# All output gates as seven-product pairs, a shorter queue of plain blocks beside the scan, and the scan's skip moved to a group's end

## The chip, the cores and the metric

The kernel runs on one core of a Trainium2 chip. The metric is the device time of one execution in microseconds, as the median of the runs; a profile of one execution comes with it. All times below are microseconds unless they are marked ns.

## The reference, cut to what matters

One layer of a hybrid decoder runs for a prompt of 1024 tokens and 8 sample tokens. The two are processed side by side as one matrix of 1032 columns (tokens), with the model dimension of 1024 on the partitions in 8 tiles of 128. Three mixers read the same normalised input through one projection `w_in`:

```python
sc_b, sc_c, sc_x, z, xbc, dt_raw, q, gates = jnp.split(xn @ w_in, splits, axis=-1)
y_a = (sc_b * conv_u) @ w_sc_out
y_ssd, ssm_new = ssd_fn(xs, dt, a, bm, cm, ssm_s0)
y_ssd = (y_ssd + ssm_d[:, None] * xs).reshape(bsz, seq, SSM_D_INNER) * jax.nn.silu(z)
y_b = group_rmsnorm(y_ssd, ssm_norm_w, SSM_GROUPS) @ w_ssm_out
y_c = jnp.einsum('bhlm,bmhd->blhd', probs, mem_v).reshape(bsz, seq, ATTN_DIM) @ w_attn_o
g_a, g_b, g_c = jnp.split(jax.nn.sigmoid(gates), N_BRANCHES, axis=-1)
merged = g_a * y_a + g_b * y_b + g_c * y_c
```

The term `ssm_d * xs` is the skip. The state-space scan (`ssd_fn`) has 4 groups of 8 heads and, for the prompt, 8 chunks of 128 tokens; the sample's tokens take a recurrent step of their own. A feed-forward part and norms follow.

## The kernel before, in words

All matrix products are of fp32 precision, made of three products of fp32r parts (`hi`, `lo`). A **block** is one tile of 128 output columns of a weight, for all 1032 tokens. It is computed in one of two forms. `gemm` (line 203 is its matmul) takes a **plain block**: 8 input tiles x 3 parts x 3 column slices of 344, 72 matmuls. `strassen` (line 248, through `st_prod`) takes a **pair** of blocks with seven half-sized products instead of eight: 168 matmuls of 258 columns. It reads sums of the input's tiles (the forms `T1`, `nT2`, `T4`, half of them in the pool `xfx`) and writes its outputs into tiles `u` of the pool `pxa`; both pools lie at the right end of the on-chip memory and are closed by `pa_stack.close()`.

Of the 24 gate blocks, `gate_pair` computes numbers 0 to 19 as ten pairs, the last of them `gate_pair(18, plain)`, which ends this part of the kernel. Each gate goes through a `Sigmoid` and is stored to `gt_d`. The sample's recurrent steps (`with_steps`) run beside the earlier pairs. Then come two queues of plain blocks, in this order:

- `fillers`: 8 blocks of the attention's query (`q_step`) and the 4 last gates (`gate_step`, 20 to 23), 12 in all;
- `outs`: 24 blocks of output projections in three rounds of 8, `wo0m` from the short convolution (`sc_d`), `wo1m` and `wo2m` from the two halves of the state-space output (`yb_d`). Eight blocks `wo3m` of the attention's output (their results are `po3m`) follow; they read `at_d`.

A queue `pend` holds small pieces of other work. `gemm` takes `pace[0]` of them per block, spread over its eight steps (one for each input tile). At the seam between two rounds, `out_ahead` loads the next round's eight input tiles and `split_act` splits them, during the last block of the round before.

**The scan** is the first such queue. For each group: load its tiles `x` and `bc`, then for each chunk three pieces (`first`, `third`/`decay`/`prep`, `second`), then `z_pieces`, `group_norm`, and the store to `yb_d`. In a chunk, `load` brings the rows `r` from `ac_d`; `prep` makes decay factors of them on ScalarE; `first` transposes (`bp`, `xp`) and multiplies `r` with `cbm`; `second` computes `po` (from the state `s`) and `py`, sums them into `yt`, and adds the skip to `x` in four small operations (line 950); `third` updates the state through `pss`. Four PSUM uses a chunk share two small buffers. `s_skip` adds the sample's skip. The tiles of the scan come from one pool `ssd`, opened at the right end after `pa_stack` is closed. The pace is `len(pend) / (len(fillers) + KD)`: the pieces are spread over 20 blocks.

**The attention** is the second queue: 69 pieces at `pace[0] = 5`, with the sample's attention, the convolution states, and last `s_back`, which writes the sample's attention result into `at_d` (its transposes are `psob`, line 1509). After it the rest of `outs` runs without pieces.

The framework orders each engine's instructions itself, by program order and by readiness in its own model; a tile whose buffer is taken waits for the last user. On an engine, and on the SP and ScalarE queues of transfers, instructions run in the order that results.

Of the kernel before, what the change touches and what calls it, by code (L numbers as in the profile page):

```python
# [9 lines left out]
F32 = mybir.dt.float32  # L10
F32R = mybir.dt.float32r
AF = mybir.ActivationFunctionType
ALU = mybir.AluOpType
# [4 lines left out]
P = 128  # L18
D = 1024
T = 1024  # L20
NS = 8
TT = T + NS
# [4 lines left out]
KD = D // P  # L27
EPS = 1e-6
LAG = 3
GROUPS = 4  # L30
HEADS = 32
HPG = 8
# [5 lines left out]
C_SCB, C_SCC, C_SCX, C_Z, C_XBC, C_DT, C_Q, C_G = 0, 1024, 2048, 3072, 5120, 8192, 8224, 9248  # L38
# [3 lines left out]
def tile_kernel(ctx: ExitStack, tc, a, o):  # L42
    nc = tc.nc
    V, S, G, PE, SY = nc.vector, nc.scalar, nc.gpsimd, nc.tensor, nc.sync
# [111 lines left out]
    def ev_tile(name, shape=(P, TT + 4), dt=F32):  # L156
        return ev.tile(list(shape), dt, tag="ev", name=name)
# [8 lines left out]
    pend = deque()  # L166
# [12 lines left out]
    pace = [3, 0.0]  # L179
# [29 lines left out]
    def wblock(w, col):  # L209
        return w[:, col : col + P].rearrange("(k p) c -> p k c", p=P)  # L210
# [174 lines left out]
    w_in = a["w_in"][0]  # L385
# [3 lines left out]

    ph1 = ExitStack()  # L390
    cn = ph1.enter_context(tc.tile_pool(name="cn", bufs=1))
    h_sc = cn.tile([P, 8, 16], F32, tag="h_sc", name="h_sc")
    h_xc = cn.tile([P, 24, 24], F32, tag="h_xc", name="h_xc")
    xn = [(act_tile("ah", f"xnh{k}"), act_tile("al", f"xnl{k}")) for k in range(KD)]
    xw = [act_tile(("ah", "al")[k % 2], f"xw{k}", F32) for k in range(KD)]
    ps_dt, ps_b0 = mm_ps("ps_dt"), mm_ps("ps_B0")
# [140 lines left out]
    dtT = cn.tile([P, 9, HEADS], F32, tag="dtT", name="dtT")  # L537
    decst = cn.tile([P, NCK, HEADS], F32, tag="decst", name="decst")
    cdec = cn.tile([P, NCK, HEADS], F32, tag="cdec", name="cdec")
    dts = cn.tile([P, 16, NS], F32, tag="dts", name="dts")  # L540
    es = cn.tile([P, 16, NS], F32, tag="es", name="es")
    dpar = cn.tile([P, 16], F32, tag="dpar", name="dpar")
    ys = cn.tile([P, 16, NS], F32, tag="ys", name="ys")
    bcs = cn.tile([P, GROUPS, NS, 2], F32, tag="bcs", name="bcs")

    dt_stack = ExitStack()
    pd_ = dt_stack.enter_context(tc.tile_pool(name="pdt", bufs=1))
# [96 lines left out]
    def proj(col, name):  # L644
        return gemm(weights(wblock(w_in, col), "w" + name), xn, "ps_" + name)
# [65 lines left out]

        return [Step(wblock(w_in, C_Q + i * P), f"wq{i}", s)]

    def gate_step(i):
        def s():
            ps = proj(C_G + i * P, f"g{i}")
            t = ev_tile(f"g{i}")
            S.activation(t3(t), flat(ps), AF.Sigmoid)
            S.dma_start(gt_d[i], t[:, :TT])

        return [Step(wblock(w_in, C_G + i * P), f"wg{i}", s)]

    def xbc_conv(ct, u, name):
        G.memset(u[:, 0:3], 0.0)
        G.tensor_copy(tail_xc[:, ct // 8, :, ct % 8], u[:, T : T + 11])
# [58 lines left out]
    def gate_pair(i, after_t3=None):  # L784
        plain_pair(C_G, gt_d, i, "G", AF.Sigmoid, None, after_t3)
# [5 lines left out]
    def b3(t, n):  # L791
        return t.rearrange("p (a b) -> p a b", a=n)

    def sp_tile(shape, tag, name, bufs=2):
        return pool["ssd"].tile(shape, F32, tag=tag, bufs=bufs, name=name)


    def bc_rows():
# [67 lines left out]
        pair()  # L866
        assert not pend

    def ssd_pieces(g, xg, bcg):
        hs = slice(g * HPG, (g + 1) * HPG)  # L870
        h0 = g * HPG
        state = {}
# [4 lines left out]

        def load(c):
            nm = f"{g}_{c}"
            r = sp_tile([P, HPG, P], "r", "r" + nm, 3)  # L880
            live[c] = r
            SY.dma_start(r, ac_d[g, c].unsqueeze(0).to_broadcast([P, HPG, P]))

# [7 lines left out]
        def load_ea(c):  # L891
            ea = None
            if c > 0:
                ea = sp_tile([P, 4, P], "ea", f"ea{g}_{c}")
                for k in range(2):
                    SY.dma_start(ea[k * 64 : (k + 1) * 64], ea_d[g, c, 4 * k : 4 * k + 4].unsqueeze(0).to_broadcast([64, 4, P]))
            return ea
# [27 lines left out]
        def second(c):  # L925
            nm = f"{g}_{c}"
            cs = slice(c * P, (c + 1) * P)
            r, ea, xdt, xdd, bT = live[c]
            yt = sp_tile([P, 4, P], "yt", "yt" + nm, 1)
            if c > 0:  # L930
                po = sm_ps("po" + nm)
                for t in range(4):
                    PE.matmul(  # L933
                        po[:, t * P : (t + 1) * P], state["s"][:, t * P : (t + 1) * P], bcg[1][:, cs],
                        start=True, stop=True,
                    )
# [12 lines left out]
            for t in range(4):  # L949
                V.scalar_tensor_tensor(  # L950
                    xg[t][:, cs], xg[t][:, cs], dpar[:, g * 4 + t : g * 4 + t + 1], yt[:, t, :],
                    op0=ALU.mult, op1=ALU.add,
                )

        def third(c):
            nm = f"{g}_{c}"
            r, ea, xdt, xdd, bT = live.pop(c)
            pss = sm_ps("pss" + nm)
            PE.matmul(pss, bT, xdd, start=True, stop=True)  # L959
            if c == 0:  # L960
                s_new = sp_tile([P, 512], "s", "s" + nm)
                ins = V.tensor_copy(s_new, pss)
            else:
                s_new = state["next"]
                ins = V.tensor_tensor(s_new, pss, s_new, op=ALU.add)  # L965
            state["s"] = s_new
            return ins.ins

        def decay(c):

            s_new = sp_tile([P, 512], "s", f"s{g}_{c}")
            G.tensor_tensor(  # L972
                b3(s_new, HPG), b3(state["s"], HPG), bc(cdec[:, c, hs].unsqueeze(2), [P, HPG, 64]),
                op=ALU.mult,
            )
            state["next"] = s_new

        def final():
            ps = sm_ps(f"psf{g}")
            for t in range(4):  # L980
                PE.transpose(ps[:, t * P : (t + 1) * P], state["s"][:, t * P : (t + 1) * P], ident)
            sf = sp_tile([P, 4, P], "yt", f"sf{g}", 1)
            S.copy(sf, b3(ps, 4))
            SY.dma_start(
                o["p_ssm"][0, 0, hs].rearrange("h p n -> (h p) n").rearrange("(t q) n -> q t n", q=P), sf
            )

        def s_skip():
            for t in range(4):
                V.scalar_tensor_tensor(  # L990
                    xg[t][:, T:TT], xg[t][:, T:TT], dpar[:, g * 4 + t : g * 4 + t + 1], ys[:, g * 4 + t, :],
                    op0=ALU.mult, op1=ALU.add,
                )

        def head():
            load(0)
# [39 lines left out]
    def z_pieces(g, xg, hold):  # L1036
        def piece(t):
            zs = hold.pop(t)
            V.tensor_mul(xg[t], xg[t], zs)
            if t == 0:  # L1040
                hold["q"] = ev_tile(f"sqa{g}")
            sqa = hold["q"]
            if t == 0:
                S.activation(sqa[:, :TT], xg[t], AF.Square)
            else:
                S.activation(zs, xg[t], AF.Square)
                V.tensor_add(sqa[:, :TT], sqa[:, :TT], zs)
# [208 lines left out]
    with_steps(3, lambda: z_pair(14))  # L1256
    with_steps(2, lambda: gate_pair(16))
    assert not steps
    rb = ev_tile("rb")
    SY.dma_start(rb[:, :TT], r_d.to_broadcast([P, TT]))  # L1260
    b12s = []
# [17 lines left out]
        for kt in range(4):  # L1279
            split_to(*xforms["T3"][kt], b12s[kt // 2][:, HS[kt % 2]])  # L1280

    gate_pair(18, plain)
    st_stack.close()
    pa_stack.close()
    pmm[0] = mm_stack.enter_context(tc.tile_pool(name="pmm1", bufs=2, space=PSUM))


    pool["ssd"] = ssd.enter_context(tc.tile_pool(name="ssd", bufs=2, side="right"))
    fillers = deque()
    for i in range(8):  # L1290
        fillers.extend(q_step(i))
    for i in range(20, 24):
        fillers.extend(gate_step(i))

    acts = []

# [65 lines left out]
        )  # L1362
    for g in range(GROUPS):
        xg, bcg, hold = groups[g]
        pieces = ssd_pieces(g, xg, bcg)
        if g > 0:
            pend.extend([lambda g=g: load_group(g), None])
        pend.extend(pieces[:-3])
        pend.append(lambda g=g, hold=hold: [z_load(g, t, hold) for t in range(2)])
        pend.extend(pieces[-3:])  # L1370
        pend.extend(z_pieces(g, xg, hold) + [None] + group_norm(g, xg, hold))
    pace[0] = len(pend) / (len(fillers) + KD)
    while fillers or pend:
        if len(fillers) == 1:
            out_ahead(sc_d)
# [25 lines left out]
    if True:  # L1401
# [194 lines left out]
        pend.extend(pieces)  # L1596
        pend.extend(states)
        pend.extend([None, s_back])
        pace[0] = 5
        while pend:  # L1600
            run_next(outs)
        pace[0] = 3
        att_stack.close()
        ph2 = ctx.enter_context(tc.tile_pool(name="ph2", bufs=1))
        assert not pend
# [339 lines left out]
```

## Time and profile before

| | |
|---|---|
| median of 3 runs | 2502.28 us (2502.19 to 2504.86) |
| the profiled execution's own time | 2503.04 us |
| its span in the profile | 2501.3 us |
| busy, share of the span | TensorE 98%, weight loads 96%, VectorE 61%, ScalarE 42%, GpSimd 5% |
| transfers | 392.08 MB, mean 157 GB/s |
| pairs before the scan; scan; attention; merge and feed-forward | to 966; 966 to 1357; 1357 to 1567; from 1567 us |

The span is what lies between the first and the last instruction of the profile; the execution's own time is 1.7 us longer. A share of busy time is a mean over stages. The rows further down are copied from the page and from answers of the trace.

### The profile page before, as it was taken

How to read it: one execution, taken by the hardware profiler on the slowest of the kernel's cores; microseconds unless marked ns; L12 is line 12 of the kernel's file. 1: busy time of each engine (PE TensorE's matmuls, PEld its weight loads, DVE VectorE, ACT ScalarE, POOL GpSimd, SP SyncE). 2: the span in 40 equal slices, each digit the busy share in tenths (PEclk: the TensorE clock that was granted, in tenths of full speed). 3: DMA queues.
4: the chain of work that ended last, by engine and by line, in shares of the span. 5: the costliest groups of instructions: out<-in, count | busy, mean ns of one | idle time of the engine just before them, and what ended most of it. 6: DMA issues, size and time to landing. Idle time of an engine off the chain costs nothing.

```text
span 2501.3 us, 44971 instructions
## 1 busy us (share of the span) xinstructions
PE 2461.6 (98%) x18714; PEld 2399.9 (96%) x18714; DVE 1519.3 (61%) x2590; ACT 1047.0 (42%) x1688; POOL 135.3 (5%) x163
## 2 busy tenths in 40 slices
PE   7999999999999999999999999999999999999998
PEld 6999999999999998999989998999999999999998
DVE  6754586777677773766866662655775545453325
ACT  6554455454545534556545441223433333341212
POOL 0300000000000000321120000000000000000000
PEclk9999999999999999999999999999999999999999
DMA  6344434344344455668867686945442222282211
GB/s 202 110 150 154 128 104 143 110 140 126 99 136 136 127 160 190 192 211 266 276 199 277 218 303 218 327 144 178 140 151 95 85 68 85 86 274 89 68 34 69
DMA packets 348331, 392.08 MB, mean 157 GB/s; under 512 B 15334, under 2 KB 285782, under 8 KB 348119
## 3 DMA queue, kind: packets, MB, share of 16 engines
q1 hardware_dynamic: 327678, 331.50, 42.1%
q10 hardware_dynamic: 20449, 57.71, 6.1%
q8 instruction: 147, 2.41, 0.4%
q14 instruction: 57, 0.47, 0.1%
HBM read 280.40 MB, written 108.98 MB: 156 GB/s over the span
## 4 chain that ended last, share of the span: by engine, by line
PE 92%; DVE 2%; DMA 2%; ACT 2%; issue 1%; SPq 0%; ACTq 0%; DVEq 0%; POOL 0%
PE po L203 14%; PE pd L203 9%; PE ps_q L203 4%; PE pm L1701 4%; PE py L941 1%; PE pss L959 1%; PE ps_g L203 1%; PE po L933 1%; PE ps_z L203 1%; PE u20m L248 1%; PE u6m L248 1%; PE g20m L248 1%; PE u18m L248 1%; PE g18m L248 1%; PE u16m L248 1%
## 5 line engine op out<-in xcount | busy, mean ns | idle before, releaser
L1843 DVE TENSOR_TENSOR x<-pd,x 128x1032 f32<-128x1032 f32 x24 | 29.6, 1231 | 131.2 <-PE pd L203 131.2
L888 ACT ACTIVATE r<-r,acum 128x128 f32<-128x128 f32 x256 | 78.8, 391 | 5.3 <-DMA r<-ac_d 4.9
L659 DVE SCALAR_TENSOR_TENSOR ax<-u,prm,ax 128x1024 f32<-128x1024 f32 x44 | 56.3, 1280 | 0.1
L920 POOL TENSOR_TENSOR xdd<-xdt,decst 128x512 f32<-128x512 f32 x32 | 38.0, 1189 | 296.5 <-DVE xdt L916 296.5
L829 ACT ACTIVATE st<-st,es 128x128 f32<-128x128 f32 x128 | 41.9, 394 | 22.4 <-DMA st<-in_state_ssm_dram 20.5
L914 DVE TENSOR_TENSOR r<-r,cbm 128x1024 f32<-128x1024 f32 x32 | 39.0, 1218 | 9.5 <-ACT r L889 9.2
L1348 DVE TENSOR_TENSOR yr<-po,yr 128x1032 f32<-128x1032 f32 x8 | 9.9, 1232 | 53.8 <-PE po L203 53.8
L913 ACT COPY bT<-bp 128x128 f32<-128x128 f32 x32 | 8.5, 265 | 79.9 <-DVE cbm L911 79.9
L831 DVE SCALAR_TENSOR_TENSOR st<-sr,dts,st 128x128 f32<-128x128 f32 x128 | 40.2, 346 | 0.4
L941 PE MATMUL py<-r,xdt 128*64 128x128 f32 x512 | 35.9, 284 | 4.4 <-issue 4.4
L937 DVE TENSOR_TENSOR yt<-po,ea 128x512 f32<-128x512 f32 x28 | 19.3, 689 | 32.5 <-PE po L933 29.7
L941 PEld LDWEIGHTS py<-r,xdt 128*64 128x64 f32 x512 | 28.1, 139 | 8.7 <-issue 5.3
L950 DVE SCALAR_TENSOR_TENSOR x<-x,dpar,yt 128x128 f32<-128x128 f32 x128 | 36.2, 345 | 0.2
L835 DVE SCALAR_TENSOR_TENSOR sr<-st,sr 128x128 f32<-128x128 f32 x128 | 35.4, 286 | 1.1
L972 POOL TENSOR_TENSOR s<-s,cdec 128x512 f32<-128x512 f32 x28 | 35.1, 1253 | 0.5 <-DVE s L965 0.4
L889 ACT ACTIVATE r<-r 128x1024 f32<-128x1024 f32 x32 | 33.9, 1060 | 0.6
L959 PE MATMUL pss<-xdd,bT 128*128 128x512 f32 x64 | 33.5, 605 | 0.0
L1708 DVE TENSOR_TENSOR x<-pm,xT 128x516 f32<-128x516 f32 x16 | 11.1, 696 | 36.4 <-PE pm L1701 36.3
L933 PE MATMUL po<-bc,s 128*128 128x128 f32 x224 | 29.5, 275 | 0.0
L933 PEld LDWEIGHTS po<-bc,s 128*128 128x128 f32 x224 | 28.4, 191 | 0.0
L1630 DVE TENSOR_TENSOR gt<-po,gt 128x1032 f32<-128x1032 f32 x8 | 9.9, 1232 | 30.6 <-PE po L203 28.8
L662 DVE SCALAR_TENSOR_TENSOR ax<-u,prm,ax 128x1032 f32<-128x1032 f32 x22 | 28.3, 1286 | 0.0
(9105 smaller groups left out, 8947.7 us busy)
## 6 DMA issues: line engine op xcount, KB each, us to landing
r<-ac_d SPq DMA_DIRECT2D x32, 512.0 KB
gt<-gt_d SPq DMA_DIRECT2D x24, 516.0 KB
xs_d<-ax ACTq DMA_DIRECT2D x22, 516.0 KB
hr<-h_d SPq DMA_DIRECT2D x22, 516.0 KB
gt_d<-G ACTq DMA_DIRECT2D x20, 516.0 KB
x<-xs_d SPq DMA_DIRECT2D x16, 516.0 KB
zs<-zs_d SPq DMA_DIRECT2D x16, 516.0 KB
yb_d<-x SPq DMA_DIRECT2D x16, 516.0 KB
```

The lines of the kernel that those rows point to most:

```text
L203: PE.matmul(ps[:, n, :CW], wt[:, ks], x[:, n * CW : (n + 1) * CW], start=(k == 0 and i == 0), stop=(k == nk - 1 and i == 2),)
L248: PE.matmul(ps[:, n, :HC], wt[:, ks], x[:, n * HC : (n + 1) * HC], start=(start and kt == 0 and i == 0), stop=(kt == 3 and i == 2), skip_g ...
L659: V.scalar_tensor_tensor(acc[:, :T], u[:, j : j + T], w[j], acc[:, :T], op0=ALU.mult, op1=ALU.add)
L829: S.activation(st[:, i], st[:, i], AF.Copy, scale=es[:, g * 4 + i, b : b + 1])
L831: V.scalar_tensor_tensor(st[:, i], rb, dts[:, g * 4 + i, b : b + 1], st[:, i], op0=ALU.mult, op1=ALU.add)
L888: S.activation(r[:, j, :], r[:, j, :], AF.Relu, scale=-1.0, bias=acum[:, c, h : h + 1])
L914: V.tensor_tensor(r, r, bc(cbm.unsqueeze(1), [P, HPG, P]), op=ALU.mult)
L920: G.tensor_tensor(b3(xdd, HPG), b3(xdt, HPG), bc(decst[:, c, hs].unsqueeze(2), [P, HPG, 64]), op=ALU.mult)
L933: PE.matmul(po[:, t * P : (t + 1) * P], state["s"][:, t * P : (t + 1) * P], bcg[1][:, cs], start=True, stop=True,)
L941: PE.matmul(py[hp : hp + 64, (h // 2) * P : (h // 2 + 1) * P], xdt[:, h * 64 : (h + 1) * 64], r[:, (h % 2) * 4 + h // 2, :], start=True, s ...
L959: PE.matmul(pss, bT, xdd, start=True, stop=True)
L1701: PE.matmul(ps[:, n, :HC], wt[:, ks], x[:, half * HT + n * HC : half * HT + (n + 1) * HC], start=(k == 0 and i == 0), stop=(k == KD - 1 an ...
```

## The change

- Gates 20 to 23 become two further pairs, `gate_pair(20)` and `gate_pair(22, plain)`; `gate_step` goes. `fillers` holds the 8 query blocks alone.
- The scan is spread over `len(fillers) + KD + 2` = 18 blocks: 8 of the query, 8 of `wo0m`, and `wo10` and `wo11`. The pace carries a small fraction and starts without a rest.
- The attention's 69 pieces are spread over all but one of the 14 blocks that are left.
- The scan's pool is three: `ssr` (the rows `r`), `ssd` (`cbm`, `bT`, `xdt`, `xdd`) and `ssy` (`ea`, `s`, and `y`), opened in this order from the right end.
- `yt` of a chunk is no tile of its own but a slice of `y`, one tile of 128x4x1032 for the group. The skip is added from it in `z_pieces`, one operation of 128x1032 for each of the four tiles; `s_skip` only copies the sample's values into `y`.
- Five small tiles of the early part move into a pool `ch` that is closed before the scan, and the final state `sf` into the shared pool `ev`.

```diff
+    ch_stack = ExitStack()
+    ch = ch_stack.enter_context(tc.tile_pool(name="ch", bufs=1))
...
-    def gate_step(i):
-        def s():
-            ps = proj(C_G + i * P, f"g{i}")
-            t = ev_tile(f"g{i}")
-            S.activation(t3(t), flat(ps), AF.Sigmoid)
-            S.dma_start(gt_d[i], t[:, :TT])
...
-            r = sp_tile([P, HPG, P], "r", "r" + nm, 3)
+            r = sp_tile([P, HPG, P], "r", "r" + nm, 3, "ssr")
...
-            yt = sp_tile([P, 4, P], "yt", "yt" + nm, 1)
+            if c == 0:
+                hold["y"] = sp_tile([P, 4, TT], "y", f"y{g}", 1, "ssy")
+            yt = hold["y"][:, :, cs]
...
-            for t in range(4):
-                V.scalar_tensor_tensor(
-                    xg[t][:, cs], xg[t][:, cs], dpar[:, g * 4 + t : g * 4 + t + 1], yt[:, t, :],
-                    op0=ALU.mult, op1=ALU.add,
-                )
...
-            sf = sp_tile([P, 4, P], "yt", f"sf{g}", 1)
+            sf = ev_tile(f"sf{g}", (P, 4, P))
...
+            V.tensor_copy(hold["y"][:, :, T:TT], ys[:, g * 4 : g * 4 + 4, :])
...
             zs = hold.pop(t)
+            V.scalar_tensor_tensor(
+                xg[t], xg[t], dpar[:, g * 4 + t : g * 4 + t + 1], hold["y"][:, t, :], op0=ALU.mult, op1=ALU.add
+            )
             V.tensor_mul(xg[t], xg[t], zs)
...
+    gate_pair(18)
+    gate_pair(20)
...
-    gate_pair(18, plain)
+    gate_pair(22, plain)
     st_stack.close()
     pa_stack.close()
+    ch_stack.close()
...
-    pool["ssd"] = ssd.enter_context(tc.tile_pool(name="ssd", bufs=2, side="right"))
+    for name in ("ssr", "ssd", "ssy"):
+        pool[name] = ssd.enter_context(tc.tile_pool(name=name, bufs=2, side="right"))
...
-    for i in range(20, 24):
-        fillers.extend(gate_step(i))
...
-    pace[0] = len(pend) / (len(fillers) + KD)
+    pace[:] = len(pend) / (len(fillers) + KD + 2) + 1e-6, 0.0
...
-        pace[0] = 5
+        pace[:] = len(pend) / (len(outs) - 1) + 1e-6, 0.0
```

## Rows read from the trace of the kernel before

**Rows 1.** The page's busy times: us, share of the span, instructions.

```profile
PE 2461.6 (98%) x18714; PEld 2399.9 (96%) x18714; DVE 1519.3 (61%) x2590; ACT 1047.0 (42%) x1688; POOL 135.3 (5%) x163
```

**Rows 2.** The chain that ended last: start, us, engine, tile, line, matmuls.

```profile
945.38 20.24 PE G18m L248 x168
...
1566.63 113.28 PE po L203 x716
```

**Rows 3.** Windows by stretch: length, busy of each engine, granted clock, DMA share, GB/s.

```profile
966.39:980.94 14.55, 14.55 (x92) 14.26 (x91) 2.12 (x3) 3.10 (x9) 1.04 (x1) 1.00 1.04 332
...
992.57:1044.67 52.10, 52.10 (x396) 46.48 (x394) 37.47 (x71) 26.36 (x65) 18.44 (x16) 1.00 0.53 160
1044.67:1079.20 34.53, 34.53 (x228) 33.48 (x229) 21.21 (x29) 17.64 (x27) 4.89 (x4) 1.00 0.86 294
...
1356.98:1566.63 209.65, 207.38 (x1392) 190.62 (x1389) 107.27 (x288) 78.39 (x167) 0.00 (x0) 1.00 0.72 243
```

**Rows 4.** The same chain at the scan's start, from 980 us on.

```profile
980.94 4.44 issue
985.38 1.97 PE py L941 x16
...
988.19 4.38 PE ps_q L203 x22
...
995.85 1.02 PE py L941 x16
```

**Rows 5.** Waits of TensorE, 966 to 1342 us: total, times, longest.

```profile
PE py L941 <- issue: 4.4, 1, 4.4
PE bp L905 <- DVE yt L937: 1.1, 2, 0.7
PE xp L909 <- DMA x<-xs_d: 0.7, 2, 0.4
```

**Rows 6.** Timeline of SP's queue: start, us, operation.

```profile
973.88 1.27 SPq L882 DMA_DIRECT2D r<-ac_d  x3
```

**Rows 7.** Timeline of ScalarE and its queue, with idle before in brackets.

```profile
966.29 0.33 ACTq L779 DMA_DIRECT2D gt_d<-G  x1
...
978.91 2.74 ACT L888 ACTIVATE r<-r,acum 128x128 f32<-128x128 f32 x9 [4.39 <-DMA r<-ac_d]
...
982.96 1.06 ACT L889 ACTIVATE r<-r 128x1024 f32<-128x1024 f32 x1
```

**Rows 8.** Timeline of VectorE at the scan's start.

```profile
973.93 0.29 DVE L911 TENSOR_TENSOR cbm<-bp,tri 128x128 f32<-128x128 f32 x1 [5.48 <-DMA gt_d<-G]
```

**Rows 9.** Timeline of VectorE in a chunk of group 1.

```profile
1087.57 1.13 DVE L950 SCALAR_TENSOR_TENSOR x<-x,dpar,yt 128x128 f32<-128x128 f32 x4
1088.62 1.22 DVE L914 TENSOR_TENSOR r<-r,cbm 128x1024 f32<-128x1024 f32 x1
```

**Rows 10.** Windows of 1 us; the granted clock is the third number from the end.

```profile
983.00:984.00 1.00, 0.00 (x0) 0.00 (x0) 0.00 (x0) 1.00 (x2) 0.00 (x0) 0.64 0.02 8
...
989.00:990.00 1.00, 1.00 (x6) 1.00 (x5) 1.00 (x2) 1.00 (x5) 0.00 (x0) 0.50 0.97 271
```

**Rows 11.** Groups of VectorE, 966 to 1342 us: busy us, mean ns | idle before.

```profile
L950 DVE SCALAR_TENSOR_TENSOR x<-x,dpar,yt 128x128 f32<-128x128 f32 x128 | 36.2, 345 | 0.2
...
L1084 DVE SCALAR_TENSOR_TENSOR x<-x,prm,sqa 128x1032 f32<-128x1032 f32 x13 | 16.0, 1288 | 5.9 <-ACT sqa L1080 5.9
```

**Rows 12.** The chain that ended last in group 1's chunks.

```profile
1084.80 0.89 PE po L933 x8
...
1091.55 0.89 PE po L933 x8
```

**Rows 13.** Timeline of TensorE at the attention's end.

```profile
1565.97 0.66 PE L1509 MATMUL psob<-ident,osr 8*128 8x8 f32 x8 [1.01 <-DMA osr<-os_d]
```

**Rows 14.** Timeline of SP's queue at the attention's end.

```profile
1573.64 0.32 SPq L1301 DMA_DIRECT2D in<-at_d  x1
```

**Rows 15.** Timeline of ScalarE, the splits of the attention's result.

```profile
1579.23 1.06 ACT L162 CAST b00h<-in 128x1032 fp32r<-128x1032 f32 x1 [2.80 <-DMA in<-at_d]
...
1599.05 1.06 ACT L162 CAST b07h<-in 128x1032 fp32r<-128x1032 f32 x1 [0.22 <-DMA in<-at_d]
```

More of the change, by code (lines that the diff above doesn't have):

```diff
@@ L391, in tile_kernel @@
     cn = ph1.enter_context(tc.tile_pool(name="cn", bufs=1))
-    h_sc = cn.tile([P, 8, 16], F32, tag="h_sc", name="h_sc")
-    h_xc = cn.tile([P, 24, 24], F32, tag="h_xc", name="h_xc")
+    ch_stack = ExitStack()
+    ch = ch_stack.enter_context(tc.tile_pool(name="ch", bufs=1))
+    h_sc = ch.tile([P, 8, 16], F32, tag="h_sc", name="h_sc")
+    h_xc = ch.tile([P, 24, 24], F32, tag="h_xc", name="h_xc")
     xn = [(act_tile("ah", f"xnh{k}"), act_tile("al", f"xnl{k}")) for k in range(KD)]
@@ L539, in tile_kernel @@
     cdec = cn.tile([P, NCK, HEADS], F32, tag="cdec", name="cdec")
-    dts = cn.tile([P, 16, NS], F32, tag="dts", name="dts")
-    es = cn.tile([P, 16, NS], F32, tag="es", name="es")
+    dts = ch.tile([P, 16, NS], F32, tag="dts", name="dts")
+    es = ch.tile([P, 16, NS], F32, tag="es", name="es")
     dpar = cn.tile([P, 16], F32, tag="dpar", name="dpar")
     ys = cn.tile([P, 16, NS], F32, tag="ys", name="ys")
-    bcs = cn.tile([P, GROUPS, NS, 2], F32, tag="bcs", name="bcs")
+    bcs = ch.tile([P, GROUPS, NS, 2], F32, tag="bcs", name="bcs")
     dt_stack = ExitStack()
@@ L712, in q_step @@
         return [Step(wblock(w_in, C_Q + i * P), f"wq{i}", s)]
-    def gate_step(i):
-        def s():
-            ps = proj(C_G + i * P, f"g{i}")
-            t = ev_tile(f"g{i}")
-            S.activation(t3(t), flat(ps), AF.Sigmoid)
-            S.dma_start(gt_d[i], t[:, :TT])
-        return [Step(wblock(w_in, C_G + i * P), f"wg{i}", s)]
     def xbc_conv(ct, u, name):
@@ L792, in b3, with sp_tile @@
         return t.rearrange("p (a b) -> p a b", a=n)
-    def sp_tile(shape, tag, name, bufs=2):
-        return pool["ssd"].tile(shape, F32, tag=tag, bufs=bufs, name=name)
+    def sp_tile(shape, tag, name, bufs=2, at="ssd"):
+        return pool[at].tile(shape, F32, tag=tag, bufs=bufs, name=name)
     def bc_rows():
@@ L867, in with_steps, with ssd_pieces @@
         assert not pend
-    def ssd_pieces(g, xg, bcg):
+    def ssd_pieces(g, xg, bcg, hold):
         hs = slice(g * HPG, (g + 1) * HPG)
@@ L893, in load_ea @@
             if c > 0:
-                ea = sp_tile([P, 4, P], "ea", f"ea{g}_{c}")
+                ea = sp_tile([P, 4, P], "ea", f"ea{g}_{c}", at="ssy")
                 for k in range(2):
@@ L960, in third @@
             if c == 0:
-                s_new = sp_tile([P, 512], "s", "s" + nm)
+                s_new = sp_tile([P, 512], "s", "s" + nm, at="ssy")
                 ins = V.tensor_copy(s_new, pss)
@@ L969, in decay @@
         def decay(c):
-            s_new = sp_tile([P, 512], "s", f"s{g}_{c}")
+            s_new = sp_tile([P, 512], "s", f"s{g}_{c}", at="ssy")
             G.tensor_tensor(
@@ L988, in s_skip @@
         def s_skip():
[L989 to L993, printed above, removed]
+            V.tensor_copy(hold["y"][:, :, T:TT], ys[:, g * 4 : g * 4 + 4, :])
         def head():
@@ L1364, in tile_kernel @@
         xg, bcg, hold = groups[g]
-        pieces = ssd_pieces(g, xg, bcg)
+        pieces = ssd_pieces(g, xg, bcg, hold)
         if g > 0:
@@ L1598, in tile_kernel @@
         pend.extend([None, s_back])
-        pace[0] = 5
+        pace[:] = len(pend) / (len(outs) - 1) + 1e-6, 0.0
         while pend:
             run_next(outs)
-        pace[0] = 3
+        pace[:] = 3, 0.0
         att_stack.close()
```

## The prediction, made before the change was run

> **What bounds the kernel now.** I read the page first, for which engine is busy [rows 1]: TensorE, 98% of the span, so time is to be had only by giving it less work or by taking away the little in which it stands. Next the chain of work that ended last, for the price of a block of columns in each form: a pair of gate blocks by the seven-product form takes 20.24 us without a gap, and 716 matmuls of plain blocks take 113.28 us, 158.2 ns each, so a plain block of 72 takes 11.39 us [rows 2]. Then busy times by stretch, over the scan (966 to 1357 us) and the attention (1357 to 1567) [rows 3]: TensorE is full in the scan's chunks (52.10 of 52.10 us), full between two groups (34.53 of 34.53), and 2.3 us short in all of the attention. The waits of TensorE between 966 and 1342 us sum to 6.2 us; 4.44 of it is one wait, before the first `py` [rows 4, 5]. That is the one large hole near this change.
>
> The hole, step by step. The last gate pair's second result goes to `gt_d` at 966.29. The first `r` load is issued at 973.88, and the first `cbm` starts at 973.93, after 5.48 us in which VectorE waited for that store [rows 6 to 8]. Both are tiles of the pool `ssd`, of different tags, and both waited for one store, so I read the wait as the whole pool's: it lies on the memory of the pairs' output tiles. ScalarE gets `r` at 978.91 and starts its `Exp` at 982.96 [rows 7]; with 1.06 us for that and 1.22 for the product with `cbm` (as in [rows 9]), `py` starts at 985.38. TensorE had stood since 980.94, and its granted clock went from 1.00 through 0.64 in the microsecond from 983 to 0.50 (of 2.4 GHz the lower level, 1.2), where it still is at 989 [rows 10]. The 16 records of `py` took 1.97 us instead of 1.02, and 22 matmuls took 4.38 instead of 22 x 0.158 = 3.48 [rows 4]. With some 0.3 us on the transposes between, the hole costs 4.44 + 0.95 + 0.90 + 0.3 = 6.6 us.
>
> **Gates as pairs.** Four plain blocks (45.56 us) leave the scan; two pairs (40.48) come before it: -5.1 us. The pairs before it show no gap [rows 2] and the added two have no sample step to hide, so I add nothing for seams. With the plain gates their four `Sigmoid` evictions and table loads leave the scan's ScalarE; that lies beside TensorE and counts nothing.
>
> **Three pools.** `r` (12 KB a partition) and then 10 KB of `cbm`, `bT`, `xdt`, `xdd` now fit in the 24.2 KB of the input's forms, the outermost pool on that side, which TensorE alone releases. Only `ea`, `s` and `y` still lie on the pairs' output tiles and wait for the store. So `r` can be issued at about 966 instead of 973.9. What it meets: the pair's two stores, a weight block and `r` itself, some 2 MB, at the 332 GB/s of that stretch [rows 3] 6.1 us: it lands at 972. From landing to the product took 985.3 - 978.9 = 6.4 us: ready at 978.5. But `py` is also due sooner: `pend` holds 41 + 3 x 39 = 158 entries, paced before over 20 blocks (7.9 a block, `second(0)` falls to the second block), now over 18 (8.78, it falls to the eighth step of the first, behind 63 matmuls, so 976.4). So about 2.1 us of waiting stays. The clock fell only after more than 2 us of standing [rows 4, 10], so I count no loss for it: 6.6 - 2.1 = -4.5 us. Bounds: -6.6 if the schedule puts `py` behind the product; +4.5 if `r` lands no sooner than before (985.3 against a place at 976.4 instead of 980.9).
>
> **The skip at a group's end.** Out go 128 operations of 345 ns, 36.2 us of VectorE as they overlap, and the small sample ones; in come 16 on 128x1032 at the 1288 ns of the same operation in the group norm, 20.6 us [rows 11]. In a chunk the four take 1.05 us (1087.57 to 1088.62), in front of the product that `xdt`, `pss` and `po` follow [rows 9]. A chunk that runs as fast as it can takes 6.75 us from `po` to `po` [rows 12], TensorE full all the while. Without the four: 5.7 us. Between two groups the four longer operations add 5.1 us and the last skip's 1.1 goes: 34.5 us become 38.5. The moved work is hidden by blocks running ahead there; its price if they ran out is those 4 us three times.
>
> Is there cover enough with two blocks fewer? From the first `py` to the end of group 3's chunks it is 1313.2 - 985.4 = 327.8 us; less two blocks (22.8) it is 305. The scan's own chain now is 32 x 5.7 + 3 x 38.5 = 298. It just fits, with 7 us over. Two seams, where eight input tiles are split for the next weights, now fall into it (before: one, and one in its tail). The one before left VectorE late for `bp` by 1.1 us, and loads made `xp` wait 0.7 [rows 5]. I take +1.0 for new waits of this sort; bounds -1.8 (those go) and +4 (a boundary uncovered).
>
> **The other pace.** Attention's 69 entries were run at 5 a block and ended in the 14th of 16 blocks; now at 69/13 in the 13th of 14. `s_back` was due at the fifth of eight steps of that block and its `psob` came at 1565.97, four matmuls into the next, 6.3 us late, with 22.1 us of blocks still ahead of the attention output's weights. Late by as much, it now falls 2.4 steps into the last block, with 5.6 x 1.42 = 8.0 us to come. Behind `psob` follow a copy, the store to `at_d`, the loads and the splits. Before, the first load was issued at 1573.64, its split began at 1579.23 and ended at 1580.3, 14.3 us after `psob`, and the eighth began at 1599.05 [rows 13 to 15]; but that load stood for a buffer, not for data. Without that: 0.9 us to the copy's end, some 2 for the store (my estimate, between nothing and the 5.6 of the load), 5.6 and 1.06: 9.5 us. So 1.5 us of waiting: +1.5, between 0 and 6.3 (if the buffer is waited for again).
>
> **Sum.** -5.1 - 4.5 + 1.0 + 1.5 = -7.1 us against the profiled execution's own 2503.0 (span 2501.3 and 1.7 around it): 2495.9. The median of the runs shown lies 0.8 us lower, so 2495.2.
>
> **Rivals.** (1) *The hole at the scan's start stays.* The stretch from 966 to 981 already moves 332 GB/s with DMA busy throughout [rows 3]: no wait is left, but the same bytes are. If `r` lands at 975 or later, behind the state-space gate loads and stores, 5 us or more of waiting stay, with the clock's fall: -5.1 + 0 + 2.5 gives 2499.7, from 2497.5 to 2504. For it: three 512 KB loads join two stores. Against: no other `r` stopped TensorE. The Trainium skill (DMA: Bandwidth & Descriptors, Issuing engines are not separate DMA queues) says that transfers issued by different engines run on the same 16 DMA engines and interleave; by that rule the loads from SP gain little by not waiting for ScalarE's stores, which speaks for this rival, and the stretch's busy DMA agrees.
>
> (2) *The scan's chain is the bound, not TensorE.* If a chunk stays at 6.75 us (some other step takes the skip's place), the chain is 32 x 6.75 + 3 x 38.5 = 331 us against 305; blocks run ahead, and what the attention doesn't make good is lost, 4 to 8 us of the 26: 2499 to 2503. For it: the period from `po` to `po` was VectorE's chain [rows 9, 12]. Against: nothing else in VectorE's order of a chunk stands where the skip stood. The Trainium skill (Perfetto Trace Analysis, Identifying the Most-Contended Engine) warns that matmul busy time misjudges TensorE and wants the weight loads' share instead; here that is 46.48 of 52.10 us in the chunks, 89%, against 97% between groups, which would leave 11% there that fewer blocks don't win.
>
> (3) *Slower: the attention output's weights wait.* If `s_back` slips past the last plain block (over 8 us more than in the sum, by a late store of the states or a scan that ends two blocks late), TensorE stands the 14.3 us to the first split and meets the other seven at (1599.1 - 1579.2) / 7 = 2.8 us each against 1.42: 9.9 more. 24.2 us lost against the 8.6 won elsewhere: 2508 to 2518. From 8.6 us of standing the change wins nothing, from 13.6 it is slower by 0.2%. Against it: `psob` came 6.3 us late before, no more.
>
> **Chances.** The forecast 0.57 (2490 to 2497.2), (1) 0.17, (2) 0.15, (3) 0.08; 0.03 that no wait is added and the whole hole goes (-11.7 - 1.8: 2488.8). To be 0.2%, 5 us, off is about what a measurement tells from no change: faster needs under 2497.3. That holds for the forecast, the best case and a little of (1) and (2): 0.62; within: 0.30, the rest of (1) and (2); slower: (3), 0.08. Leaving out the best case, (3) and the tops of (1) and (2), 0.2 in all, the range is 2489.5 to 2502.
>
> **What would show it.** Right: the first `r` load issued by 967 with no wait on `gt_d`; TensorE's wait before the first `py` under 2.5 us and no half clock there; twelve gate pairs of 20.2 us; chunks of 5.7 to 6 us where they run free; `psob` before or early in the last block `wo27`, and under 2 us of wait at the first matmul of `po30`. Wrong: a wait of 4 us or more before `py`; waits on the splits `b00` to `b07` in a seam that meets the four long skips; TensorE standing at `po30`; or chunks still at 6.7 us.

## The result, and the profile after

The changed kernel takes 2506.84 us (median of 17 runs, 2503.57 to 2511.44) against 2503.15 for the kernel before on the same chip (17 runs): ratio 1.0017, 95% interval 1.001 to 1.0024, so 4 us slower, where 7 us faster were forecast. The profiled execution took 2510.98 us, span 2509.3, 4 us above its median. That is kept in mind where its waits are added up.

The page's busy times, and the chain of work that ended last (start, us, matmuls), which answer to [rows 1, 2]:

```profile
PE 2463.0 (98%) x18762; PEld 2398.2 (96%) x18762; DVE 1518.3 (61%) x2484; ACT 1047.5 (42%) x1694; POOL 128.2 (5%) x163
```

```profile
967.21 20.23 PE G20m L248 x168
987.44 20.24 PE G22m L248 x168
...
1594.48 93.69 PE po L203 x576
```

The two new pairs cost what was forecast. TensorE has less work (four plain blocks out, two pairs in), yet its busy time is no lower: time at the low clock counts as busy too. From the start of `G18m` to the start of `pm` the kernel before took 734.53 us (945.38 to 1679.91) and this one 741.20 (946.97 to 1688.17).

The scan's start, which answers to [rows 4, 6, 7]: SP's queue, then the chain.

```profile
1006.26 1.31 SPq L875 DMA_DIRECT2D r<-ac_d  x3
```

```profile
1008.43 7.98 DMA gt_d<-G
...
1017.04 2.73 DMA ea<-ea_d
```

The first `r` is issued 1.4 us before the last pair ends (at 1007.68); only `ea` still waits for the pair's store (`gt_d<-G`). The waits of TensorE from 980 to 1700 us (total, times, longest) show no `py`:

```profile
PE po L203 <- ACT b00h L162: 4.4, 1, 4.4
PE pskT L1413 <- DMA kk<-k_d: 3.3, 1, 3.3
PE pss_sc L1460 <- ACT ot L1561: 1.5, 1, 1.5
PE xp L902 <- DMA x<-xs_d: 0.8, 1, 0.8
```

Instead there are two new waits, one at either end of the attention. Here are windows (columns as in [rows 3]) of the scan's start and of these two ends:

```profile
1015.00:1025.00 10.00, 9.66 (x68) 8.52 (x68) 5.64 (x7) 9.74 (x20) 0.33 (x1) 1.00 0.84 259
...
1375.00:1385.00 10.00, 6.65 (x31) 6.44 (x30) 7.29 (x8) 7.51 (x10) 0.00 (x0) 0.66 1.02 340
...
1585.00:1595.00 10.00, 5.62 (x35) 5.32 (x34) 5.23 (x6) 2.44 (x3) 0.00 (x0) 0.91 0.90 305
1595.00:1605.00 10.00, 10.00 (x50) 9.81 (x49) 7.46 (x7) 6.09 (x7) 0.00 (x0) 0.74 0.93 319
```

From 1595 to 1605 TensorE is busy throughout, but with 50 matmuls where 10 us at 158.2 ns hold 63: the clock, granted at 0.74 on average, costs 2 us behind the wait of 4.4. The same happens behind the wait for `kk`, the keys. The chain there:

```profile
1368.39 0.32 SPq L1076
...
1368.80 0.70 SPq L1087
...
1369.60 0.55 SPq L1408
...
1371.57 7.50 DMA kk<-k_d
1379.06 0.14 issue
1379.20 1.94 PE pskT L1413 x8
```

SP issues the last group's four stores to `yb_d` (L1076), then the sample's queries (L1087), and only then the keys `kk` (L1408). The transposes `pskT` of the first load run at 1374.82 without a wait; the second load, issued at 1371.57, takes 7.50 us, and TensorE stands 3.3 us for it. In the kernel before nothing waited here:

```profile
1350.35 0.47 SPq L1416 DMA_DIRECT2D kk<-k_d  x1
```

```profile
1356.82 1.04 PE L1421 MATMUL pskT<-ident,kk 128*128 128x128 f32 x8
```

The four stores stood ahead of the keys there too (from 1342.95). But from the last transposes of the scan's end (`psqr`) to `pskT`, TensorE had 15.3 us of other matmuls before, and has 11.1 now. At the other end, the place of [rows 13, 14, 15]: TensorE, SP, ScalarE.

```profile
1584.49 0.66 PE L1501 MATMUL psob<-ident,osr 8*128 8x8 f32 x8
```

```profile
1586.03 0.37 SPq L1503 DMA_DIRECT2D at_d<-o_s  x1
...
1588.50 11.35 SPq L1293 DMA_DIRECT2D in<-at_d  x8
```

```profile
1593.37 1.05 ACT L162 CAST b00h<-in 128x1032 fp32r<-128x1032 f32 x1 [0.19 <-DMA in<-at_d]
```

From `psob` to the first split it is 8.9 us, to that split's end 9.9, and the plain blocks end at 1590.1.

To compare stretches I use one measure: for each window of 10 us from 940 to 1700, the time TensorE was idle plus its busy time times one minus the granted clock. Summed, this "loss" is 12.2 us before (6.3 of it the hole) and 20.9 after: 5.1 up to 1360, mostly in the scan, against 3.6 besides the hole, and 15.8 from 1360 on, in the attention and at `po30`, against 2.3. The windows give the clock to two digits only, so a difference of a microsecond in this sum says little.

### The profile page after: what moved, and what is told of

Read it like the earlier page. It is cut to its first block, busy times and chain, and to the rows that moved or that the text cites. A ratio compares the mean times of both kernels' runs of the same rounds, so it can differ in the third digit from the quotient of the medians.

```text
span 2509.3 us, 44975 instructions
## 1 busy us (share of the span) xinstructions
PE 2463.0 (98%) x18762; PEld 2398.2 (96%) x18762; DVE 1518.3 (61%) x2484; ACT 1047.5 (42%) x1694; POOL 128.2 (5%) x163
## 4 chain that ended last, share of the span: by engine, by line
PE 89%; DMA 4%; DVE 2%; ACT 2%; issue 1%; SPq 0%; ACTq 0%; POOL 0%; DVEq 0%
PE po L203 13%; PE pd L203 9%; PE pm L1693 4%; PE ps_q L203 2%; PE pss L949 1%; PE py L936 1%; PE po L928 1%; PE ps_z L203 1%; PE u20m L248 1%; PE C3m L248 1%; PE Z6m L248 1%; PE g20m L248 1%; PE u18m L248 1%; PE g18m L248 1%; PE u16m L248 1%
## 5 line engine op out<-in xcount | busy, mean ns | idle before, releaser
L932 DVE TENSOR_TENSOR y<-po,ea 128x512 f32<-128x512 f32 x28 | 19.3, 688 | 28.0 <-PE po L928 25.1
L1700 DVE TENSOR_TENSOR x<-pm,xT 128x516 f32<-128x516 f32 x16 | 11.1, 695 | 36.3 <-PE pm L1693 36.3
L1073 DVE SCALAR_TENSOR_TENSOR x<-x,prm,sqa 128x1032 f32<-128x1032 f32 x16 | 19.6, 1290 | 15.0 <-ACT sqa L1069 15.0
```

## Experiments

Theory T: the forecast gains came, and were given back at the two ends of the attention, since fewer plain blocks run beside it. Rival R1: the loss lies in the scan, in its seams and the long skips. Rival R2: the pools or the skip cost by themselves. The table gives for each kernel the plain blocks allotted to the scan and the attention (in brackets the number over which the attention's pieces are spread, where that is set by the number), the ratio to the kernel before in the same session, and the loss.

| kernel | pairs | blocks | ratio (95%) | loss, us |
|---|---|---|---|---|
| before | 10 | 20 + 16 | 1 | 12.2 |
| changed | 12 | 18 + 14 (13) | 1.0017 (1.0010 to 1.0024) | 20.9 |
| e11 pools alone | 10 | 20 + 16 | 0.9973 (0.9964 to 0.9982) | 4.8 |
| e1 pools and skip | 10 | 20 + 16 | 0.9983 (0.9974 to 0.9993) | 5.4 |
| e2 pairs and paces | 12 | 18 + 14 (13) | 1.0050 (1.0037 to 1.0064) | 24.2 |
| e12 all but the skip | 12 | 18 + 14 (13) | 1.0045 (1.0031 to 1.0059) | 20.0 |
| e8 changed, 12 | 12 | 18 + 14 (12) | 0.9995 (0.9986 to 1.0004) | 11.7 |
| e3 changed, 11 | 12 | 18 + 14 (11) | 1.0026 (1.0015 to 1.0037) | 16.4 |
| e4 states earlier | 12 | 18 + 14 (13) | 1.0044 (1.0031 to 1.0056) | 24.2 |
| e6 loads ahead | 12 | 18 + 14 (13) | 1.0022 (1.0012 to 1.0033) | 18.1 |
| e10 as e8, keys first | 12 | 18 + 14 (12) | 1.0004 (0.9995 to 1.0013) | 14.9 |
| e7 changed, shifted | 12 | 17 + 15 (13) | 1.0080 (1.0066 to 1.0094) | 34.0 |
| e5 eleven pairs | 11 | 18 + 16 | 0.9998 (0.9989 to 1.0007) | 13.0 |
| e9 eleven pairs | 11 | 19 + 15 (13) | 1.0081 (1.0067 to 1.0095) | 30.2 |
| e13 eleven pairs | 11 | 17 + 17 | 1.0128 (1.0108 to 1.0148) | 49.9 |
| e14 as e13, skip in the chunk | 11 | 17 + 17 | 1.0131 (1.0114 to 1.0147) | 48.1 |

**The parts of the change, one by one.** First the pools and the skip without the pairs and with the two old paces (e1):

```diff
-    gate_pair(22, plain)
+    gate_pair(18, plain)
...
+    for i in range(20, 24):
+        fillers.extend(gate_step(i))
```

> The three pools and the moved skip alone: gates 20 to 23 stay plain blocks in the queue beside the scan, the scan stays spread over 20 blocks and the attention at 5 pieces a block. Theory T (the forecast gains came, and were given back at the two ends of the attention because fewer blocks run there): the hole before the first py goes (-6.3 us) and neither end of the attention changes, so 6 us under the kernel before, about 2497; no wait above 1.5 us at pskT, none at po30. Rival R1 (the loss lies in the scan, in its seams and the long skips at a group's end): the long skips are here too, so no faster than the kernel before, 2502 to 2506. Rival R2 (the pools or the skip themselves cost): 2503 or more, with the hole still there in part.

The hole goes (no wait for `py`), and neither end of the attention waits for `kk` or `b00h`: the longest wait from 960 to 1700 us is 1.6 (at `pskT`, for VectorE's `kTl`). That is 4.3 us faster than before (1.7 to 6.5); T had given 6, and R1 and R2 no gain. The reverse (e2), the pairs and both paces on the kernel before:

```diff
-    gate_pair(18, plain)
+    gate_pair(18)
+    gate_pair(20)
...
+    gate_pair(22, plain)
...
-    pace[0] = len(pend) / (len(fillers) + KD)
+    pace[:] = len(pend) / (len(fillers) + KD + 2) + 1e-6, 0.0
...
-        pace[0] = 5
+        pace[:] = len(pend) / (len(outs) - 1) + 1e-6, 0.0
```

> The pairs and the two paces of the changed kernel alone, with the old single pool and the skip in each chunk. T: the pairs give -5.1 us, the hole at the scan's start stays (0 to +4.5, since py is due sooner), the chunks keep their 6.75 us so that the scan's 298 us of chain become 331 against 305 us of blocks, and both ends of the attention lose at least what they lose in the changed kernel (12.8 us): 2511 to 2520, slower than the changed kernel's 2506.8. R1 (loss by the long skips): they are not here, so 2498 to 2503. R2 (pools or skip cost): 2498 to 2503 as well, with the ends of the attention free of waits.

12.5 us slower, within what T gave. Its waits:

```profile
PE po L203 <- ACT b00h L162: 4.7, 1, 4.7
PE py L932 <- issue: 4.1, 1, 4.1
PE pskT L1412 <- DMA kk<-k_d: 3.6, 2, 2.1
```

The hole and both ends are there, and no long skip is. So the ends are the doing of the pairs (fewer blocks) and the paces together; no run parts these two. Then the pools alone, with the skip in each chunk (e11: `yt` is again a tile of its own, in `ssy`, and the four small operations stand behind it):

> The kernel before with the three pools and the pool that is closed early, and nothing else: the skip stays in each chunk. T: the hole before the first py goes and nothing else changes: the ratio of the kernel with pools and skip, 0.9975 to 0.999. If the moved skip carries part of that gain (a chunk's shorter chain), 0.9990 to 1.0.

0.9973: the pools carry the whole measured gain, and this is the lowest ratio of the study (its interval overlaps that of e1), 6.8 us (4.5 to 9.0) under the kernel before. And the changed kernel with only the skip put back (e12):

```diff
-            if c == 0:
-                hold["y"] = sp_tile([P, 4, TT], "y", f"y{g}", 1, "ssy")
-            yt = hold["y"][:, :, cs]
+            yt = sp_tile([P, 4, P], "yt", "yt" + nm, 1, "ssy")
...
+            for t in range(4):
+                V.scalar_tensor_tensor(
+                    xg[t][:, cs], xg[t][:, cs], dpar[:, g * 4 + t : g * 4 + t + 1], yt[:, t, :],
+                    op0=ALU.mult, op1=ALU.add,
+                )
```

> The changed kernel with the skip put back into each chunk: pairs, paces and pools of the changed kernel. T: the scan's chain is 6.75 us a chunk again, which the pairs-only kernel shows to cost about 3 us of scan, to be paid at the attention's start; the hole stays closed: ratio 1.0025 to 1.004, between the changed kernel's 1.0017 and the pairs-only 1.005. R1 (the four long skips at a group's end are what costs): faster than the changed kernel, ratio under 1.0005.

1.0045, just above what T gave: by the ratios the moved skip is worth 7 us in the changed kernel, where blocks are short, and nothing clear of noise beside 20 blocks (e1 against e11). The two profiles don't show where: from `G18m` to `pm` they differ by 1 us, and the loss is not higher in e12; the changed kernel's profiled execution was 4 us above its median, and that of e12 2 us below. R1 in the form "the long skips cost" falls. So does R2, by e1 and e11.

**The attention's end.** e3 and e8 change one number, so that `s_back` comes two blocks (e3, shown) or one block (e8, with 2 for the 3) sooner:

```diff
-        pace[:] = len(pend) / (len(outs) - 1) + 1e-6, 0.0
+        pace[:] = len(pend) / (len(outs) - 3) + 1e-6, 0.0
```

> The changed kernel with the attention's 69 pieces spread over all but three of its 14 blocks instead of all but one (6.3 a block instead of 5.3), so that s_back comes two blocks, 22.8 us, sooner. T: the wait at po30 and its half clock go, -6 to -7 us against the changed kernel's 2506.8, so 2500; the wait at pskT stays. If denser pieces make new waits inside the attention, they eat part: up to 2503. R1 and R2: the end of the attention costs little, so 2505 to 2507 with the wait at po30 gone and the time found elsewhere.

> The changed kernel with the attention's 69 pieces over all but two of its 14 blocks (5.75 a block, between the changed kernel's 5.3 and the 6.3 of the run with all but three), s_back one block sooner. T: the wait at po30 goes (-7), and the denser pieces bring about half of the waits inside the attention that 6.3 a block brought (those were 4.3 us for vc, 3.0 for ot, each with the clock's fall behind it), so -7 + 5 = -2: ratio 1.0005 to 1.002. If the waits inside come at a threshold that 5.75 doesn't reach: ratio 0.999. R1: as the changed kernel, 1.0015 to 1.002, whatever the waits do.

In both the wait at `po30` is gone. In e8 `psob` and the first split come while plain blocks still run:

```profile
1571.96 0.66 PE L1501 MATMUL psob<-ident,osr 8*128 8x8 f32 x8
```

```profile
1582.77 1.05 ACT L162 CAST b00h<-in 128x1032 fp32r<-128x1032 f32 x1 [10.99 <-DMA in<-at_d]
```

5.5 us are won against the changed kernel (2.2 in 1000), between the two cases given. e3 wins nothing and is slower than either theory gave; as many microseconds come back inside the attention:

```profile
PE pso L1484 <- DMA vc<-in_cache_mem_v_dram: 4.3, 1, 4.3
PE psv L1558 <- ACT ot L1561: 3.0, 1, 3.0
```

e4 tried to bring `psob` forward by putting the four convolution states ahead of the last pieces of the sample's attention:

```diff
-        pend.extend(pieces)
-        pend.extend(states)
+        at_ = len(pieces) - 2 * NS - 2
+        pend.extend(pieces[:at_] + states + pieces[at_:])
```

> The changed kernel with the four pieces of the convolution states put ahead of the last pieces of the sample's attention instead of behind them, so that the load of the sample's result isn't behind their stores; pace unchanged. T: psob comes some 4 to 6 us sooner, the wait at po30 shrinks from 4.4 us to about nothing with its half clock: -4 to -6 us against the changed kernel's 2506.8, 2501 to 2503. If at_d's own way (store, load, split) sets the end and not the states, no change: 2506 to 2507. R1 and R2: no change as well, since the end of the attention is not where the loss is.

The forecast was wrong: `psob` came 2.3 us later, at 1586.82, the plain blocks ended 2.6 us sooner, and the wait grew:

```profile
PE po L203 <- ACT b00h L162: 9.6, 1, 9.6
```

The states are in the way to `psob` all the same, as SP's queue suggests, first in the changed kernel and then in e4:

```profile
1571.51 1.10 SPq L1494 DMA_DIRECT2D os_d<-so  x4
...
1578.57 0.30 SPq L1498 DMA_DIRECT2D osr<-os_d  x1
```

```profile
1577.76 1.10 SPq L1494 DMA_DIRECT2D os_d<-so  x4
...
1579.95 0.86 SPq L1498 DMA_DIRECT2D osr<-os_d  x1
```

From the last stores of the sample's result to the load that feeds `psob` it is 7.1 us with the states between, and 2.2 without; and in the changed kernel's chain a state's store of 5.98 us stands ahead of the store to `at_d`. But four pieces put ahead, at 5.3 a block, delay the sample's own last pieces by more: the last `pso` fell from 1570.36 to 1576.61.

**The attention's start.** e6 gives the loads of keys and values a piece of their own, two pieces ahead:

```diff
-        pieces = [[(kv_in, 0)], [(kv_in, 1), (a_load, 0)], [], []]
+        pieces = [[(kv_load, 0), (kv_load, 1)], [], [(kv_in, 0)], [(kv_in, 1), (a_load, 0)], [], []]
```

> The changed kernel with the loads of the attention's keys and values in a piece of their own, two pieces ahead of the transposes pskT that read them (71 pieces spread over the same 13 blocks, so s_back keeps its place). T: the wait for kk at pskT (3.3 us) and its half clock go: -4 to -5.5 us against the changed kernel, ratio 0.9995 to 1.0002; the wait at po30 stays. If TensorE waits instead at the first use of the keys, psa, nothing is won: ratio 1.0015 or more. R1: no change, 1.0015 or more.

Nothing won. The keys kept their place in SP's order behind the stores (issued at 1368.99 and 1371.57), so TensorE still waited 2.4 us for `kk`, and 2.4 us for `ot` later. e10 (on e8) loads both keys before both values:

```diff
-        pieces = [[(kv_in, 0)], [(kv_in, 1), (a_load, 0)], [], []]
+        pieces = [[(k_load, 0), (k_load, 1), (k_in, 0)], [(k_in, 1), (a_load, 0)], [(v_in, 0)], [(v_in, 1)]]
```

> The kernel with the attention over all but two of its blocks (ratio 0.9995), and the keys' two loads ahead of the values' two, so that the first kk takes the buffer that the first vv had (issued at 1353, not at 1368 behind the last group's stores). T: the wait of 3 us for kk and the clock's fall behind it go, -3 to -4.5: ratio 0.9978 to 0.9985. Rival: the same wait moves to the second kk or to psa, and nothing is won: 0.999 to 1.0005.

Now the wait for `kk` is gone, and there are others in its place, among them this one; the waits at `psp`, `psv` and for `vc` add 1.8 us to what they were in e8:

```profile
PE psa L1533 <- ACT q00h L162: 1.7, 1, 1.7
```

The rival holds: nothing is won by moving one load. That the whole start of the attention comes too soon behind the scan's end fits this, but is argued and not shown.

**Where the blocks lie.** T said that blocks shifted between scan and attention trade one loss for another. e7 shifts one block to the attention, at the same density there:

```diff
-    pace[:] = len(pend) / (len(fillers) + KD + 2) + 1e-6, 0.0
+    pace[:] = len(pend) / (len(fillers) + KD + 1) + 1e-6, 0.0
...
-        pace[:] = len(pend) / (len(outs) - 1) + 1e-6, 0.0
+        pace[:] = len(pend) / (len(outs) - 2) + 1e-6, 0.0
```

> The changed kernel with one block shifted from the scan to the attention: the scan's pieces spread over 17 blocks, the attention's over all but two of 15, so at the same 5.3 a block, with s_back one block, 11.4 us, sooner before po30. T: the wait at po30 and its half clock go, -7 us; the scan's own chain (298 us by the prediction) is 4 us longer than its 294 us of blocks then, which costs 0 to +4: together -3 to -7 against the changed kernel, ratio 0.999 to 1.0005. R1 (the scan's seams and long skips set the time): a shorter scan makes it slower, ratio 1.002 to 1.005.

Much slower than either theory gave, though the wait at `po30` is gone:

```profile
PE psv L1558 <- ACT ot L1561: 5.8, 1, 5.8
PE psny L1049 <- DVE sqa L1036: 5.8, 1, 5.8
```

e5 takes one more pair than e1 and two plain blocks fewer, with the paces of the kernel before (the edit is against e1); e9 shares the same blocks out as 19 and 15:

```diff
+    gate_pair(18)
...
-    gate_pair(18, plain)
+    gate_pair(20, plain)
...
-    for i in range(20, 24):
+    for i in range(22, 24):
```

> The pools and the skip with one further pair only: gates 20 and 21 become the eleventh pair, 22 and 23 stay plain blocks, so that the scan has 18 blocks beside it as in the changed kernel and the attention keeps its 16 blocks at 5 pieces each. T (the loss is the attention's cover of 14 blocks): the hole's 6.3 us and 2.5 us for the pair are kept, no wait at po30, none above 2 us at pskT: ratio to the kernel before 0.996 to 0.9975, about 2.5 us below the kernel with pools and skip alone. R1 (the loss lies in the scan, which has 18 blocks here too, with the same seams and long skips): ratio 1.000 or more.

> Eleven pairs with 34 plain blocks, shared out as 19 for the scan and 15 for the attention (its 69 pieces over 13 of them, 5.3 a block, s_back two blocks before the end). The kernel with 18 and 16 had ratio 0.9998, with its loss inside the scan. T in its widened form (each end and the scan lose as soon as their cover is short): the scan's loss shrinks by about half of the 7 us that 18 instead of 20 blocks cost, the attention's 15 blocks cost 1 to 2: ratio 0.9985 to 0.9995. Rival (the loss in the scan is a chance meeting of splits and long skips at a seam, not cover): no trend, 0.999 to 1.002.

e5 has the attention's cover of the kernel before and none of the two waits, but loses inside the scan; its ratio is near where R1 had it, so T alone is not enough. e9, with more cover for the scan, is slower than either side gave. It loses 14.9 us in the scan against 9.7 in e5, and 14.7 more in the attention, where its longest wait is one of 5.5 us at `psv` for `ot`, as in e7. In the scan both lose most in one place; windows of e5 and of e9:

```profile
1165.00:1195.00 30.00, 26.54 (x175) 23.45 (x173) 22.70 (x26) 24.79 (x46) 7.10 (x4) 0.94 0.93 327
```

```profile
1165.00:1195.00 30.00, 20.16 (x119) 17.36 (x119) 16.34 (x20) 14.71 (x24) 1.04 (x1) 0.83 0.80 292
```

With 11 pairs the seam between the queries' and gates' blocks and `wo00` lies after block 10; spread over 18 or 19 blocks, the second group ends at about 9.0 or 9.5. In e9 the chain runs through both:

```profile
1171.61 1.23 DVE b02l L163
1172.83 3.62 DVE x L1082 x3
...
1176.47 0.32 SPq L1085
...
1176.84 0.46 SPq L1268
...
1177.34 6.03 DMA bc<-xs_d
...
1183.41 0.81 PE bp L908 x2
```

VectorE splits the next weights' inputs (`b02l`) between the group's norm products (L1082), their stores to `yb_d` (L1085) hold the next group's loads on SP (L1268), and TensorE waits for `bc`. Theory S was formed from this: the scan loses where a seam meets a group's end. With 17 blocks the end moves to 8.5, away from the seam, while cover shrinks. e13 and e14 (with the skip in the chunk) test it:

```diff
-    pace[0] = len(pend) / (len(fillers) + KD)
+    pace[:] = len(pend) / (len(fillers) + KD - 1) + 1e-6, 0.0
```

> Eleven pairs and 34 plain blocks with pools and moved skip, shared out as 17 for the scan and 17 for the attention at 5 pieces a block. With 18 for the scan a group's end (at 9.0 blocks) lay just ahead of the seam after block 10 and cost 5 us there, with 19 (9.5 blocks) 12.6 us; with 17 it lies at 8.5. Theory S (what is lost in the scan is lost where a seam's splits meet a group's end, and not by cover): the loss at that seam falls under 2 us, ratio 0.9965 to 0.9985, in spite of the shorter scan. Rival C (cover alone: 17 blocks are 294 us against 298 of chain): slower than with 18, ratio 1.0005 or more, with waits all through the scan.

> The same shares with the skip in each chunk, as in the kernel with the pools alone (ratio 0.9973). S: the pair's 2.5 us come on top, less what the chunk's longer chain (6.75 us, 331 us against 294 of blocks) takes: 0.9965 to 0.9985. C: that chain can't be run in 17 blocks' time, TensorE waits inside the scan for some 10 us or more: 1.001 or more.

Both ratios are on C's side, and far beyond it. The waits inside the scan that C gave are there in part: up to 1330 us e13 loses 13.2 us, against 9.7 in e5, while e14, for which C had given 10 or more, loses 5.0 up to 1320. More lies behind the scan. Windows of e13:

```profile
1165.00:1195.00 30.00, 28.41 (x207) 25.62 (x206) 23.15 (x26) 24.87 (x44) 7.97 (x5) 1.00 0.94 322
1340.00:1370.00 30.00, 9.49 (x40) 7.84 (x39) 14.46 (x14) 9.96 (x13) 0.00 (x0) 0.60 0.89 300
```

At the old place less than 2 us are lost, with less cover, so there S was right, though the rest of the scan lost more. But the next seam, after block 18, now stands right behind the scan's end at 17, where the attention starts, and 20 us of waiting with the clock at 0.60 follow, which S had not foreseen either. A meeting by itself does not decide: in the kernel before and in e5 a seam lies right at the scan's end (after blocks 20 and 18), and no more than 1.7 us are lost from 1340 to 1370. The chain of e13 there:

```profile
1345.07 0.61 SPq L1303
...
1345.73 6.94 DMA vv<-v_d
...
1353.89 1.24 DVE vl L1416
...
1355.15 3.46 DMA vv<-v_d
```

Two input tiles of the seam (`in`, L1303), the first values `vv`, the first keys and others all come from `ev_tile`, whose five buffers they share. The second `vv` is issued at 1355.15, 0.02 us after the last reader of the first (`vl`) ends, and TensorE waits up to 13.2 us at one time for `kk`. In e7 it is the same pool: ScalarE's copy into `ot`, another of its tiles, starts at 1471.13 when the store `yr_d<-yr` of 9.58 us ends. A sixth buffer wasn't tried, so that the pool is the cause is read from these chains and not shown by a run.

## Why the prediction was wrong, point by point

- **Gates as pairs, -5.1:** the price was right: 20.23 and 20.24 us each, no seam. That 5.1 us came of it is reckoned from the prices; no run shows it alone, and e5 with its eleventh pair was not faster than e1.
- **Three pools, -4.5 (from -6.6):** right, and a little more came: the profile shows 0.3 us of waiting where 2.1 were left standing, and the pools alone gave 6.8 us (4.5 to 9.0). Rival 1 falls. The Trainium skill (DMA: Bandwidth & Descriptors, Issuing engines are not separate DMA queues) holds that transfers of all issuing engines interleave on the same 16 engines, which spoke for rival 1; the traces don't contradict it (DMA share 0.84 from 1015 to 1025), but the wait had been one for memory, not for transport.
- **The skip:** chunks that run free take 5.8 to 5.9 us from `po` to `po` (1117.70, 1123.60, 1129.53), near the 5.7 forecast. Rival 2 falls.
- **The scan's new waits, +1.0 (-1.8 to +4):** 1.5 by the loss measure, within the bounds. But the argument behind it, 305 us of blocks against 298 of chain, was too coarse: e5 and e9 lose 5 and 13 us at one seam that this sum doesn't see. If it is the meeting with a group's end that costs there, as S has it, the changed kernel was spared by luck (its second group ends at 9, its seam lies at 8); the prediction had not worked that out.
- **The other pace, +1.5 (0 to 6.3):** this is the step that failed, in two ways. At `po30` the wait was 4.4 us and the low clock behind it 2, at the upper bound: `psob` fell not 2.4 but 4.7 steps into `wo27` (which began at 1577.78), and the prediction had counted no clock for a wait of this size. The way from `psob` to the split's end, 9.9 us, was near the 9.5 forecast. e8 shows 5.5 us to be had there. And the attention's start had no term at all: TensorE now reaches the keys' transposes 11.1 us behind the scan's last ones instead of 15.3, while the keys are issued behind the last group's stores (3.3 us of waiting, and about as much again of low clock). `ot` adds 1.5. Together the attention and `po30` lost 13.5 us more than before, where +1.5 stood.
- **The sum:** -5.1, -6.3, +1.5 and +13.5 make +3.6, near the 4 us measured between medians. That is partly luck: the losses are read from the profiled executions, and between these the stretch is 6.7 us longer, which leaves 3 us that I don't place.
- **Rival 3** (slower, by the attention output's weights) named one of the two places, but not the size: 6.4 us there is below the 8.6 from which it would have decided. The kernel is slower because a second wait, at the attention's other end, joined it.

T holds for the changed kernel itself: most of what was lost lies at the attention's two ends, and moving one of them (e8) wins back as much as the kernel lost. It does not hold as a rule about the number of blocks, as e7, e9 and e13 show; where the boundaries fall counts too.

What stays open: whether e5's and the changed kernel's remaining small waits have one cause, and how much of the wait for `kk` is SP's order and how much the five buffers; e10 moved the one and met others. Why the moved skip is worth 7 us in the changed kernel is open as well.

## What to carry to other kernels

Plain blocks of a matrix queue are cover as well as work. Before taking some away, ask at each boundary (start and end of the side work, seams, group ends) what is next on each in-order queue and in each shared pool, and how many microseconds of other matmuls stand in front of it; a sum over the whole stage can fit while each end stands. Change one part at a time: here one of the three parts carried all of the measured gain, and the kernel with that part alone is 6.8 us faster than the one before, while all together are 4 us slower.

## What the runs showed of the hardware

A wait of TensorE cost more than its own length here: 2 us behind the 4.4 at `po30`, about 3 behind the 3.3 for `kk`. The granted clock stays at the lower level for some microseconds while TensorE is busy again (50 matmuls instead of 63 in 10 us). And the clock can fall with no wait at all: in the changed kernel, 18 one-column matmuls `psny` take 2.10 us from 1180.70, and from 1184 on, with TensorE busy all the time, it is granted at 0.50:

```profile
1182.00:1184.00 2.00, 2.00 (x16) 2.00 (x16) 0.88 (x6) 0.21 (x1) 0.00 (x0) 0.92 0.87 301
1184.00:1186.00 2.00, 2.00 (x9) 2.00 (x9) 0.11 (x1) 0.00 (x0) 0.00 (x0) 0.50 1.02 411
```

The same 18 matmuls at 1090.86 left it at 1.00, so what tips it isn't shown here.
